# A hybrid decoder trunk whose instructions on all engines but TensorE are ordered by latest times counted back from TensorE's products

## Chip, cores, metric

One core of one Trainium2 chip runs the whole program. The metric is the device time of one execution in microseconds (us), as the median of several.

## The reference

Two layers of a decoder trunk, with 1024 channels and 256 tokens in float32. Each normalises the stream, projects it once to 12832 channels, and feeds three mixers: a Mamba-2 scan behind a causal convolution, attention over a sliding window of 128 with sinks, and attention with a learned forgetting. Each mixer has a SiLU gate and a projection; a sigmoid gate per channel, computed from the input, merges them, and an output projection is added to the stream.

```
h = rms_norm(x, norm_w[l])
u = h @ w_in[l]                       # 1024 x 12832, all branches
ys = [mamba2(conv(xbc), z, dt, ...), swa(rope(q), rope(k), v, z, sinks), fox(q, k, v, f, z)]
g = sigmoid(u_gate + gate_bias[l])    # per branch and channel
x = x + sum(g[b] * (ys[b] @ w_proj[l, b])) @ w_out[l]
...
out = rms_norm(x, final_norm_w)
```

## The kernel before

**Weights.** The weights stream from HBM in 255 parts of at most 512 KB (128 partitions x 1024 numbers), all started by SyncE (`load_part`, L366). ScalarE rounds each part to TensorE's fast format (`hi`, L290), VectorE subtracts to get what is left (`lo`, L291), and TensorE adds three products, hi x hi, lo x hi and hi x lo (`mm`, L109). In the head, parts are split in halves (`w_high` L1470, `w_low` L1476). Six raw parts and six split ones fit; `feed` lets at most four split parts be held ahead of TensorE.

**Work of TensorE.** Every piece of the program is a function that issues the products of one set of columns, and then calls `pump`, which lets pieces that wait (`launch`) go on: scans, softmaxes and gate evictions, each with a delay in TensorE time written out by hand (`D_SOFT`, `D_FOLD`, ...). So the order of TensorE's instructions is that of the program text and of these delays. Transposes go through TensorE too (`transpose`, L113). PSUM has three banks `mm` for products and five banks `mx` for the rest.

**Order of the others.** In the head (from L1431) the order on TensorE, VectorE, ScalarE and GpSimd is that of the program text, and behind it only TensorE's is (`manual_schedule`). The rest is placed by the language's scheduler, under hints: `issue_after` (an instruction not ahead of another), `high_priority`, `keep_in_program_order` (here `pin`), and `after_evictions(3, f)`, which puts a piece behind the third eviction from now. Buffers rotate: each tag has so many, taken in turn.

**The head.** SyncE starts the first half of x (two transfers), the first weight part (two), the second part, the second half of x (512 KB, L1433), the third part, the rope table (L1435) and more parts. TensorE transposes x four blocks at a time (`turn`), VectorE multiplies with the norm's weight on the way out (L1457), ScalarE rounds to `hTh` (`high`, L1461), VectorE takes the rest (`low`, L1465); ScalarE also sums the squares (`square`, L241). The first product is that of the attention's keys (`keys`).

**What else the steps touch.** In a sliding-window quad (four heads, `swa_quad`, `attn_quad`) VectorE masks scores and takes minima (L621 to L642), ScalarE exponentiates (L616), VectorE multiplies by the reciprocal sum (L645), two heads at a time, and TensorE transposes the result. A gate's product is evicted by VectorE with a bias (`u_gate`, L1112), which ScalarE's queue has brought as a broadcast of 256 KB (L1108). A convolution channel (`u_conv`) is evicted by ScalarE in two halves (`dma_sum`, L492 and L493), a transfer that GpSimd starts adds one to the other in SBUF (L494), and then ScalarE reads the sum for the first tap (L832), VectorE for the other three (L835).

## Time and profile before

| | us |
|---|---|
| median of 3 runs | 806.49 (806.43 to 806.95) |
| profiled execution | 806.35 |
| its span | 804.6 |
| TensorE busy | 795.5 |
| VectorE busy | 684.2 |
| ScalarE busy | 534.5 |
| GpSimd busy | 167.6 |

The span runs from the first to the last instruction that the profiler records; 1.75 us of the profiled execution lie around it. Times in the trace count from the start of the span. PE is TensorE's products, PEld its loads of weights, which overlap them; DVE is VectorE, ACT ScalarE, POOL GpSimd, SP SyncE. A name with a q (SPq) is the engine's queue of instructions, where transfers are started.

### The profile page before, as it was taken

How to read it: one execution, taken by the hardware profiler on the slowest of the kernel's cores; microseconds unless marked ns; L12 is line 12 of the kernel's file. 1: busy time of each engine (PE TensorE's matmuls, PEld its weight loads, DVE VectorE, ACT ScalarE, POOL GpSimd, SP SyncE). 2: the span in 40 equal slices, each digit the busy share in tenths (PEclk: the TensorE clock that was granted, in tenths of full speed). 3: DMA queues.
4: the chain of work that ended last, by engine and by line, in shares of the span. 5: the costliest groups of instructions: out<-in, count | busy, mean ns of one | idle time of the engine just before them, and what ended most of it. 6: DMA issues, size and time to landing. Idle time of an engine off the chain costs nothing.

```text
span 804.6 us, 14840 instructions
## 1 busy us (share of the span) xinstructions
PE 795.5 (99%) x5160; PEld 710.4 (88%) x5160; DVE 684.2 (85%) x1416; ACT 534.5 (66%) x1146; POOL 167.6 (21%) x236
## 2 busy tenths in 40 slices
PE   8999999999999999999999999999999999999996
PEld 7999988888998988888998899888889988888896
DVE  6878999997998997795785899999889999969865
ACT  7776768865775885543665688687657768755452
POOL 3066213140220100033001741122311120002000
PEclk9999999999999999999999999999999999999999
DMA  9997987797756565677678987679976546587632
GB/s 309 283 260 178 251 220 201 216 298 219 197 180 169 169 190 174 216 254 206 219 251 259 238 213 211 159 217 283 284 214 204 173 144 202 158 250 208 211 108 77
DMA packets 138826, 170.43 MB, mean 212 GB/s; under 512 B 9352, under 2 KB 106464, under 8 KB 138752
## 3 DMA queue, kind: packets, MB, share of 16 engines
q1 hardware_dynamic: 114960, 140.53, 56.0%
q0 software_dynamic: 13328, 13.29, 10.5%
q10 hardware_dynamic: 10464, 15.67, 6.8%
q8 instruction: 41, 0.67, 0.3%
q14 instruction: 33, 0.27, 0.1%
HBM read 154.71 MB, written 2.16 MB: 195 GB/s over the span
## 4 chain that ended last, share of the span: by engine, by line
PE 96%; DVE 2%; DMA 1%; issue 1%; ACT 1%; SPq 0%; DVEq 0%; ACTq 0%
PE mm L109 83%; PE mx L109 9%; PE mx L113 3%; DMA raw<-in_w_in_dram 1%; DVE lo L291 0%; DVE L L1112 0%; DVE pp L621 0%; ACT hi L290 0%; DVE L L835 0%; SPq L366 0%; SPq L189 0%; DVE L L949 0%; DVE mx L629 0%; DVE L L1457 0%; ACT pp L616 0%
## 5 line engine op out<-in xcount | busy, mean ns | idle before, releaser
L109 PE MATMUL mm<-L,hi 128*128 128x512 f32 x1056 | 354.5, 387 | 0.2
L291 DVE TENSOR_TENSOR lo<-raw,hi 128x1024 fp32r<-128x1024 f32 (+1 forms) x276 | 313.2, 1153 | 40.9 <-ACT hi L290 36.1
L109 PE MATMUL mm<-hi,L 128*128 128x512 f32 (+2 forms) x1168 | 302.9, 349 | 0.1
L290 ACT ACTIVATE hi<-raw 128x1024 fp32r<-128x1024 f32 (+1 forms) x276 | 265.9, 983 | 51.1 <-PE mm L109 35.7
L109 PE MATMUL mm<-L,lo 128*128 128x256 f32 x1056 | 266.6, 273 | 0.0
L109 PEld LDWEIGHTS mm<-hi,L 128*128 128x128 f32 x1168 | 205.9, 190 | 22.9 <-issue 1.5
L109 PEld LDWEIGHTS mm<-L,hi 128*128 128x128 f32 x1056 | 195.1, 190 | 26.8 <-issue 2.4
L109 PEld LDWEIGHTS mm<-L,lo 128*128 128x128 f32 x1056 | 202.1, 191 | 5.3
L109 PE MATMUL mm<-lo,L 128*128 128x512 f32 (+2 forms) x584 | 201.3, 347 | 0.0
L109 PEld LDWEIGHTS mm<-lo,L 128*128 128x128 f32 x584 | 110.2, 190 | 11.0 <-DVE lo L291 0.3
L494 POOL DMA_DIRECT2D L<-L x68 | 60.9, 917 | 191.6 <-ACT L L493 139.5
L1080 POOL TENSOR_SCALAR_AFFINE_SELECT bias<-bias 128x128 f32<-128x128 f32 x64 | 31.9, 531 | 83.3 <-DMA bias<-cumd 82.1
L835 DVE SCALAR_TENSOR_TENSOR L<-L,vec,L 128x255 f32<-128x255 f32 (+2 forms) x96 | 46.2, 482 | 1.5
L492 ACT ACTIVATE L<-mm 128x256 f32<-128x256 f32 x84 | 32.1, 383 | 19.3 <-PE mm L109 13.9
L658 ACT ACTIVATE pp<-pp,nm 128x128 f32<-128x128 f32 x64 | 28.3, 443 | 22.9 <-DVE nm L652 22.9
L1115 ACT ACTIVATE L<-L 128x512 f32<-128x512 f32 x24 | 15.1, 631 | 34.5 <-DVE L L1112 30.7
L494 POOL DMA_DIRECT2D qt<-L x16 | 14.2, 926 | 71.8 <-ACT qt L493 65.0
L616 ACT ACTIVATE pp<-pp,nm 128x128 f32<-128x128 f32 x32 | 12.6, 394 | 24.4 <-DVE nm L621 23.6
L493 ACT ACTIVATE L<-mm 128x256 f32<-128x256 f32 x68 | 26.3, 387 | 2.0 <-DMA L<-L 2.0
L1148 POOL TENSOR_TENSOR L<-L,L 128x512 f32<-128x512 f32 x8 | 12.0, 1495 | 74.0 <-DVE L L1147 74.0
L1112 DVE TENSOR_TENSOR L<-mm,L 128x512 f32<-128x512 f32 x22 | 15.1, 687 | 11.1 <-PE mm L109 11.1
L841 ACT ACTIVATE L<-L 128x256 f32<-128x256 f32 x32 | 13.4, 418 | 16.1 <-DVE L L835 16.0
(213 smaller groups left out, 916.6 us busy)
## 6 DMA issues: line engine op xcount, KB each, us to landing
raw<-in_w_in_dram SPq DMA_DIRECT2D x191, 512.0 KB, 5.1
raw<-in_w_proj_dram SPq DMA_DIRECT2D x48, 512.0 KB, 6.1
L<-L POOLq DMA_DIRECT2D x72, 128.0 KB, 5.6
raw<-in_w_out_dram SPq DMA_DIRECT2D x16, 512.0 KB, 5.3
bias<-cumd ACTq DMA_DIRECT2D x16, 256.0 KB, 3.5
L<-cumd ACTq DMA_DIRECT2D x8, 512.0 KB, 5.9
L<-in_gate_bias_dram ACTq DMA_DIRECT2D x12, 256.0 KB, 5.2
qt<-L POOLq DMA_DIRECT2D x16, 128.0 KB, 6.0
```

The costliest lines, as they stand in the source:

```text
L109: nc.tensor.matmul(o, a, b, **kw)
L113: nc.tensor.transpose(o, a, i)
L290: keep(act)(hi, src, AF.Copy)
L291: keep(tt)(lo, src, hi.bitcast(F32), op=ALU.subtract)
L492: act(halves(lo), ordered(p[:, S:2 * S]), AF.Copy)
L493: last = act(halves(out), ordered(p[:, 0:S]), AF.Copy)
L494: nc.gpsimd.dma_start(out, lo, accum_op=ALU.add)
L658: act(pp[:, i, sl], pp[:, i, sl], AF.Exp, scale=-1.0, bias=nm[:, e:e + 1], accum_out=sums[:, e:e + 1])
L835: stt(a[:, s:S], x_[:, 0:S - s], y.vec[:, 16 * j + u:16 * j + u + 1], a[:, s:S], op0=ALU.mult, op1=ALU.add)
L1080: nc.gpsimd.affine_select(out=bias[:, i, dst], in_=bias[:, i, src], compare_op=ALU.is_ge, fill=NEG, base=0, pattern=[[-1, P]], channel_mul ...
L1112: tt(halves(g), p, halves(y.gb), op=ALU.add)
L1115: finish(act(g, g, AF.Tanh, scale=0.5))
```

## The change

The program text stays, but `nc` is now a recorder: every call adds an `Op` with what it reads and writes, and nothing is issued. At the end `order_of` gives each op a latest time, counted back from the times at which TensorE would do its products if it never waited (`deadlines`). It then plays all five engines through with a time for each kind of instruction and transfer (`Op.cost`, `run`): at each step an engine takes, of the ops that can start first, the one with the earliest latest time. A buffer goes to who is ready first, in the slot that is free first. Behind the first 16 us an op steps back if another with an earlier time would be held up by it (`guarded`). The loop runs four times, with TensorE's times taken anew from the last round. `emit` then issues everything in the order found, on all engines by hand, so every instruction has line 461, and each slot is a tile of its own.

The hints `issue_after`, `high_priority` and `keep_in_program_order` are gone. The identity matrix is made by a memset and a select instead of a helper that does the same. TensorE's instructions and their order are the same in both kernels, as are the numbers of the other engines' compute instructions. The core of the diff:

```diff
+def deadlines(ops, before, end):
+    for op in ops:
+        op.late = op.nominal + op.busy if op.engine == "tensor" else end + 50.0
+    for op in reversed(ops):
+        op.due = min(op.nominal, op.late - op.busy) if op.engine == "tensor" else op.late - op.busy
+        for d in op.deps:
+            o = ops[d]
+            o.late = min(o.late, op.due - (3.0 if o.dma else o.lag))
...
+            c = [(max(r, free[e]), op) for r, op in c if r is not None]
...
+            t0 = min(r for r, _ in c)
+            r, op = min(((r, op) for r, op in c if r <= t0 + 1e-9), key=lambda x: (x[1].due, x[1].i))
+            if e != "tensor" and not forced and t0 > OPENING:
+                until = guarded(e, t0, op)
...
+        if op.dma:
+            wire = max(wire, op.end + 0.8) + op.kb / 330
+            op.land = max(wire + 1.0, op.end + 2.2)
...
+    with tc.manual_schedule(engines={ENG.PE, ENG.DVE, ENG.Activation, ENG.Pool, ENG.SP}):
+        for op in order:
...
+            getattr(getattr(nc, op.engine), op.name)(*map(real, op.args), **{k: real(v) for k, v in op.kw.items()})
...
-        with tc.issue_after(out.ins):
+        if True:
             for _ in range(len(ends_later)):
                 ends_later.pop(0)()
...
-                with tc.high_priority():
+                if True:
...
-    with tc.manual_schedule(engines={ENG.PE}):
-        for g in late:
-            g()
-        for i, f, last in ops[3:]:
-            run_op(i, f, last)
+    for g in late:
+        g()
+    for i, f, last in ops[3:]:
+        run_op(i, f, last)
+
+    bufs_of = {tag: n for tag, (_, n, _, _) in nc.space.items()}
+    emit(nc, order_of(nc, bufs_of, verbose=VERBOSE), tc, pools)
```

Three places where the order moves. The first is ScalarE's queue in the head. Before, from the first square on (`ss` takes the sums; `L8_23_128` is `hTh`, the rounded x; `hi_...` the weight parts):

```order
L241 ACTIVATE L2_36_141,ss_25_130<-L8_3_68 128x512
L1461 ACTIVATE L8_23_128<-L8_22_127 128x512
L1470 ACTIVATE hi_26_131<-raw_12_99 128x512 x2
L1461 ACTIVATE L8_23_128<-L8_22_127 128x512
L1470 ACTIVATE hi_28_133<-raw_13_102 128x512 x2
L241 ACTIVATE L2_41_209,ss_25_130<-L8_3_68 128x512
L1461 ACTIVATE L8_23_128<-L8_22_127 128x512 x2
L1470 ACTIVATE hi_30_135<-raw_15_107 128x512 x2
L241 ACTIVATE L2_42_247,ss_25_130<-L8_3_68 128x512
L241 ACTIVATE L2_43_249,ss_25_130<-L8_3_68 128x512
```

And now, where `L8_2_2_132` is `hTh` and `in_gate_bias_dram` the gate's bias in HBM:

```order
L461 ACTIVATE tab_0_0_67<-tab_0_0_67 128x1
L461 ACTIVATE L2_1_0_111,ss_0_0_112<-L8_0_0_69 128x512
L461 ACTIVATE L8_2_2_132<-L8_1_1_125 128x512
L461 ACTIVATE L2_2_1_139,ss_0_0_112<-L8_0_0_69 128x512
L461 ACTIVATE hi_0_0_153<-raw_0_0_86 128x512
L461 DMA L2_3_10_162<-in_gate_bias_dram 128x512
L461 ACTIVATE hi_0_0_153<-raw_0_0_86 128x512
L461 ACTIVATE L8_2_2_132<-L8_1_1_125 128x512
L461 ACTIVATE hi_1_1_184<-raw_1_1_97 128x512 x2
L461 ACTIVATE L2_4_2_207,ss_0_0_112<-L8_0_0_69 128x512
L461 ACTIVATE L2_5_3_217,ss_0_0_112<-L8_0_0_69 128x512
L461 ACTIVATE L8_2_2_132<-L8_1_1_125 128x512
```

The sums of the second half of x (`L2_4_2_207`, `L2_5_3_217`) moved from behind both L1461 of that half to ahead of them, and a gate-bias transfer now stands between the halves of the first high copy. A first such transfer stands further ahead, as ScalarE's third instruction, behind the transfer of norm_w; before, the first is the 31st row of the queue. On GpSimd the transfers of the small constants of both layers now alternate with the masks right behind the identity; before, those of layer 0 alone stand there, behind the masks and the root of L224. On SyncE the rope table moved back by three weight parts.

The second place is VectorE's queue in layer 0 around the end of the fourth sliding-window quad and the eviction of the second token half of a gate. Before (`pp_399_1959` and `pp_400_1960` are the two pairs of heads, `L2_426_2086` the gate):

```order
L1112 TENSOR_TENSOR L2_411_2031<-mm_398_1946,L2_397_1944 128x512
L644 RECIPROCAL rsum_408_2009<-sums_402_1962 128x4
L642 TENSOR_TENSOR sums_402_1962<-sums_402_1962,es_409_2012 128x4
L645 TENSOR_TENSOR pp_399_1959<-pp_399_1959,rsum_408_2009 128x2x256
L644 RECIPROCAL rsum_410_2016<-sums_402_1962 128x4
L645 TENSOR_TENSOR pp_400_1960<-pp_400_1960,rsum_410_2016 128x2x256
L949 SCALAR_TENSOR_TENSOR L8_184_909<-L1_412_2034,L8_184_909 128x256
L291 TENSOR_TENSOR lo_421_2069<-raw_373_1841,hi_420_2068 128x1024
L291 TENSOR_TENSOR lo_424_2081<-raw_376_1855,hi_423_2080 128x1024
L291 TENSOR_TENSOR lo_439_2143<-raw_390_1918,hi_438_2142 128x1024
L1112 TENSOR_TENSOR L2_426_2086<-mm_413_2037,L2_397_1944 128x512
L291 TENSOR_TENSOR lo_442_2157<-raw_393_1932,hi_441_2156 128x1024
```

And now (`pp_1_7_2082` is the second pair, `L2_5_12_2120` the gate, `vec_0_0_937` the taps' weights):

```order
L461 TENSOR_TENSOR es_1_7_2075<-nm_1_3_2004,nsink_0_0_316 128x4
L461 SCALAR_TENSOR_TENSOR L1_2_102_1979<-L1_5_94_1920,vec_0_0_937,L1_2_102_1979 128x255
L461 SCALAR_TENSOR_TENSOR L1_6_96_1905<-L1_12_86_1796,vec_0_0_937,L1_6_96_1905 128x253
L461 SCALAR_TENSOR_TENSOR L1_2_102_1979<-L1_5_94_1920,vec_0_0_937,L1_2_102_1979 128x254
L461 TENSOR_TENSOR lo_2_50_2089<-raw_2_50_1812,hi_2_50_2072 128x1024
L461 TENSOR_TENSOR lo_3_51_2098<-raw_3_51_1851,hi_3_51_2087 128x1024
L461 TENSOR_TENSOR sums_1_3_2017<-sums_1_3_2017,es_1_7_2075 128x4
L461 SCALAR_TENSOR_TENSOR L1_2_102_1979<-L1_5_94_1920,vec_0_0_937,L1_2_102_1979 128x253
L461 TENSOR_TENSOR L2_5_12_2120<-mm_1_41_2056,L2_3_10_162 128x512
L461 RECIPROCAL rsum_3_7_2128<-sums_1_3_2017 128x4
L461 TENSOR_TENSOR lo_4_52_2130<-raw_4_52_1889,hi_4_52_2109 128x1024
L461 TENSOR_TENSOR pp_1_7_2082<-pp_1_7_2082,rsum_3_7_2128 128x2x256
```

The first pair's multiplication (`pp_0_6`) stands five rows ahead of these. The second pair's moved from ahead of three splits to behind three, and taps of the convolution stand among them; the gate's eviction moved from behind the third of these splits to behind the second. All four quads of a layer show the same: the first pair is multiplied before the second's minima have all been taken, and the second pair follows behind splits and taps.

The third place is ScalarE's queue at the first tap of a convolution channel in layer 0. Before, the eviction of `L1_227_1100`, to which the transfer adds, stands seven rows ahead of these, and the last row reads it:

```order
L290 ACTIVATE hi_252_1234<-raw_208_1025 128x816
L1045 ACTIVATE L8_64_331<-mm_244_1170 128x136
L1046 ACTIVATE L8_64_331<-mm_244_1170 128x120
L948 ACTIVATE L1_245_1197<-L8_184_909 128x256
L290 ACTIVATE hi_256_1254<-raw_220_1076 128x816
L290 ACTIVATE hi_278_1360<-raw_223_1090 128x544
L290 ACTIVATE hi_281_1374<-raw_238_1147 128x1024
L1045 ACTIVATE L8_64_331<-mm_248_1209 128x136
L1046 ACTIVATE L8_64_331<-mm_248_1209 128x120
L832 ACTIVATE L1_255_1248<-L1_227_1100,vec_180_898 128x256
```

And now, where the second row is the eviction of `L1_7_53_1150` and the last one reads it:

```order
L461 ACTIVATE L1_5_52_1144<-mm_0_21_1111 128x256
L461 ACTIVATE L1_7_53_1150<-mm_0_21_1111 128x256
L461 ACTIVATE L4_0_0_1156<-mx_1_14_1141 128x512
L461 ACTIVATE hi_0_30_1166<-raw_0_30_933 128x1024
L461 ACTIVATE L1_11_57_1174<-L8_0_6_967 128x256
L461 ACTIVATE L1_9_58_1181<-L8_0_6_967 128x256
L461 ACTIVATE L1_0_55_1186<-mm_2_22_1148 128x256
L461 ACTIVATE L1_1_56_1190<-mm_2_22_1148 128x256
L461 ACTIVATE hi_1_31_1195<-raw_1_31_963 128x816
L461 ACTIVATE L1_6_59_1208<-L1_7_53_1150,vec_0_0_937 128x256
```

Between eviction and reader 15 rows stood before, and 7 stand now.

More of the change, by code (lines that the diff above doesn't have):

```diff
@@ L9 @@
 from concourse._compat import with_exitstack
-from concourse.masks import make_identity
 F32 = mybir.dt.float32
@@ L47, with __init__ @@
 C_G = 9760
+ENG = mybir.EngineType
+ENGINES = ("tensor", "vector", "scalar", "gpsimd", "sync")
+FIRST_WRITES = ("out", "accum_out")
+SLIP, OPENING = 0.05, 16.0
+class Buf:
+    def __init__(self, tag, shape, dtype, space):
+        self.tag, self.shape, self.dtype, self.space = tag, list(shape), dtype, space
+        self.on_p = space != "dram"
+        free = shape[1:] if self.on_p else shape
+        self.n = int(np.prod(free)) if len(free) else 1
+        self.ap = None
+        self.turn = None
+        self.users, self.open, self.last = [], 0, 0.0
+        self.writer = np.full((4, self.n), -1, np.int32)
+        self.pe_reader = np.full((4, self.n), -1, np.int32)
+        self.readers = []
@@ new lines, in finish_of, with order_of @@
+def finish_of(op):
+    return op.land if op.dma else op.end + op.lag
+def order_of(rec, bufs_of, rounds=4, verbose=False):
+    ops = rec.ops
+    by_tag = {}
+    for b in rec.bufs:
+        by_tag.setdefault(b.tag, []).append(b)
+    for op in ops:
+        op.behind = [d for d in op.behind - op.deps if ops[d].engine != "tensor" or op.engine != "tensor"]
+        op.deps = sorted(op.deps)
+        for d in op.deps:
+            ops[d].after.append((op, True))
+        for d in op.behind:
+            ops[d].after.append((op, False))
+    before = {}
+    for tag, bs in by_tag.items():
+        n = bufs_of[tag]
+        for a, b in zip(bs, bs[n:]):
+            before[id(b)] = a
+    t = 0.0
+    for op in ops:
+        if op.engine == "tensor":
+            op.nominal = t
+            t += op.busy
+    end = t
+    for _ in range(rounds):
+        deadlines(ops, before, end)
+        end, before = run(ops, by_tag, bufs_of)
+        t = 0.0
+        for op in ops:
+            if op.engine == "tensor":
+                t = op.start if op.start < OPENING else t
+                op.nominal = t
+                t += op.busy
+        end = t + 8.0
+        if verbose:
+            print("end", round(end, 1))
+    return sorted(ops, key=lambda op: (op.start, op.i))
@@ L190, in hybrid_trunk @@
     ident = T("ident", [P, P])
-    make_identity(nc, ident)
+    nc.gpsimd.memset(ident, 0.0)
+    nc.gpsimd.affine_select(out=ident, in_=ident, compare_op=ALU.not_equal, fill=1.0, base=0,
+                            pattern=[[-1, P]], channel_multiplier=1)
     tri = T("tri", [P, P])
@@ L881, in ssd_group @@
         decs = []
-        with tc.issue_after(own.ins):
+        if True:
             ds = T("ds", [P, 4], bufs=2)
@@ L1427, in tables @@
                 act(cs[32 * r:32 * r + 32, i, :], p[src, 0:S], AF.Copy)
-    ENG = mybir.EngineType
-    with tc.manual_schedule(engines={ENG.PE, ENG.DVE, ENG.Activation, ENG.Pool}):
+    if True:
         load_to(2)
```

328 lines of the change are left out of this document (307 added, 21 removed).

## Prediction

> **What bounds the kernel now.** I read the page first, then the busy time of each engine by stretch (head, body, tail), then the waits of TensorE, then the chain of waits. The page's first line gives the span, and the stretches give TensorE's share in each.
>
> ```profile
> span 804.6 us, 14840 instructions
> ```
>
> Columns of the next rows: stretch, its length, busy us of PE, PEld, DVE, ACT and POOL, granted clock, DMA share, GB/s.
>
> ```profile
> 0.00:12.64 12.64, 10.19 (x63) 8.57 (x63) 7.44 (x14) 7.70 (x15) 2.36 (x15) 1.00 0.86 275
> 12.64:798.30 785.66, 785.34 (x5098) 701.86 (x5098) 674.41 (x1395) 525.94 (x1130) 165.20 (x221) 1.00 0.74 212
> 798.30:804.60 6.30, 0.00 (x0) 0.00 (x0) 2.38 (x9) 0.82 (x2) 0.00 (x0) 0.69 0.22 83
> ```
>
> TensorE works 785.34 of the 785.66 us between 12.64 and 798.30. It idles 2.45 us ahead of that and 6.30 us behind it; in the body 0.32 us. The change leaves TensorE's instructions and their order as they are, so all that it can give is these idle times, and all that it can cost is new ones. Its waits by releaser:
>
> ```profile
> PE mx L113 <- POOL ident masks.py:199: 1.5, 1, 1.5
> PE mx L113 <- DMA L<-in_x_dram: 0.3, 1, 0.3
> PE mx L109 <- ACT hi L1470: 0.3, 2, 0.2
> ```
>
> All three are in the head. The chain of waits there (start, us, what) shows which transfer sets the moment from which TensorE runs through:
>
> ```profile
> 2.69 5.61 DMA raw<-in_w_in_dram
> ...
> 10.02 0.45 PE mx L113 x4
> 10.47 0.02 issue
> 10.50 0.70 DVE L L1457
> 11.20 0.02 issue
> 11.22 0.64 ACT L L1461
> 11.87 0.04 issue
> 11.91 0.71 PE mm L109 x4
> ```
>
> The second weight part lands at 2.69 + 5.61 = 8.30, TensorE works on it until 10.02, then transposes the second half of the tokens; VectorE and ScalarE turn these into operands, and at 11.91 the first of the long products starts. From there on TensorE has no slack, so whatever moves 11.91 moves the end by as much.
>
> The profiled execution took 806.35 us, 0.14 under the median of the runs shown, 806.49. I make the sum in differences, and lay it on the median.
>
> **The head.** In the new order ScalarE starts two gate-bias transfers of 256 KB in the opening (behind norm_w, and between the two halves of the first high copy); before, the first of them starts at 23.5 us (last row below). GpSimd starts the small transfers of both layers at once, where before those of layer 0 start behind the root. SyncE's order is the same but for the rope table, moved back behind three weight parts. What these meet:
>
> ```profile
> 3.21 0.50 SPq L1433 DMA_DIRECT2D L<-in_x_dram  x1
> L<-in_x_dram SPq DMA_DIRECT2D x1, 512.0 KB, 6.4
> DMA packets 2641, 2.87 MB, mean 358 GB/s; under 512 B 98, under 2 KB 2402, under 8 KB 2641
> L<-in_gate_bias_dram ACTq DMA_DIRECT2D x1, 256.0 KB, 6.1
> L1108 ACTq DMA_DIRECT2D L<-in_gate_bias_dram x12: 334/352/444, 23.5 to 741.6; - x12
> ```
>
> The third row is the traffic of 8 to 16 us, when the DMA engines are busy throughout. The second half of x, issued at 3.21, lands at 3.21 + 6.4 = 9.6. At 358 GB/s each 256 KB (262 thousand bytes) takes 0.73 us from whoever is behind it. The first gate-bias transfer is issued ahead of the weights and of x; the second at about 7 us, and a landing 6.1 us after the issue, as the fourth row has it, would let most of it share the engines while x is under way. I count both in full, 1.46 us: x at 11.07.
>
> The small transfers have a price in two adjacent stretches, of which the second is when before's eight of layer 0 land:
>
> ```profile
> 18.00:20.00 2.00, 2.00 (x21) 2.00 (x20) 1.95 (x2) 2.00 (x8) 2.00 (x5) 1.00 1.03 365
> 20.00:22.00 2.00, 2.00 (x20) 2.00 (x19) 1.12 (x1) 2.00 (x3) 0.52 (x1) 1.00 1.00 242
> ```
>
> The DMA share stays at 1.00 while the rate falls from 365 to 242 GB/s: 246 thousand bytes less in 2 us, worth 0.67 us at 365. Of the new thirteen, those issued by 5 us can land ahead of x, perhaps half of them. Bounds 0 and 0.67; I take 0, since the first ones are issued behind the masks and weights already stand in the queue, and keep 0.67 for the range.
>
> Then ScalarE. Both squares of the second token half now stand ahead of L1461 of that half; before, they come later.
>
> ```profile
> L241 ACT ACTIVATE L<-L x14: 398/616/632, 3.8 to 796.3; 128x512 f32<-128x512 f32 x8, 128x256 f32<-128x256 f32 x6
> L241 ACT ACTIVATION_READ_ACCUMULATOR L<-L x14: 184/188/190, 4.4 to 796.9; 128x1 f32 x14
> ```
>
> A square with its read of the sum is 0.62 + 0.19, less some overlap: 0.75, two of them 1.5. They wait for x, so they end at 11.07 + 1.5 = 12.57, and L1461 follows there and not at 11.22: **+1.35 us**. VectorE's part isn't later: the transposes need x at 11.07 too, + 0.48 + 0.70 makes 12.25. With only the first transfer in the way x lands at 10.33, the squares end at 11.83: +0.6. With the small transfers as well: +2.0. With the early transfers free: 9.6 + 1.5 = 11.1, which 11.22 covers: 0. So 0 to +2.0.
>
> [...]
>
> **The body.** There VectorE is what TensorE stands closest to.
>
> ```profile
> 45.00:190.00 145.00, 144.81 (x1002) 129.72 (x1002) 130.98 (x288) 104.50 (x258) 50.92 (x63) 1.00 0.89 236
> 100.00:152.00 52.00, 51.81 (x366) 45.45 (x365) 50.31 (x131) 39.05 (x103) 10.92 (x14) 1.00 0.75 203
> 200.00:300.00 100.00, 100.00 (x742) 89.40 (x741) 94.35 (x252) 74.36 (x181) 14.40 (x28) 1.00 0.65 185
> ```
>
> Between 100 and 152 us VectorE is busy 50.31 of 52. There TensorE loses 0.19 of its 0.32 us, at two places of that stretch: the transposes of a quad's probabilities, and a product behind a gate's eviction.
>
> ```profile
> 123.08 0.69 DVE L645 TENSOR_TENSOR pp<-pp,rsum 128x512 f32<-128x512 f32 x1
> 123.92 0.63 PE L113 MATMUL mx<-ident,pp 128*128 128x128 f32 x4
> 129.62 0.60 PE L113 MATMUL mx<-ident,pp 128*128 128x128 f32 x4
> 145.48 0.69 DVE L645 TENSOR_TENSOR pp<-pp,rsum 128x512 f32<-128x512 f32 x1
> 146.09 0.42 DVE L949 SCALAR_TENSOR_TENSOR L<-L,L 128x256 f32<-128x256 f32 x1
> 146.50 3.50 DVE L291 TENSOR_TENSOR lo<-raw,hi 128x1024 fp32r<-128x1024 f32 x3
> 149.91 0.68 DVE L1112 TENSOR_TENSOR L<-mm,L 128x512 f32<-128x512 f32 x1
> 150.74 1.33 PE mm L109 x7
> ```
>
> The first pair of heads is normalised until 123.77 and transposed at 123.92: no slack. The second pair is wanted 5.7 us later. Before, VectorE does both pairs of a quad together; the new order finishes the first, and puts two splits and some taps ahead of the second. That is some 2 us less work ahead of the first (minima, sums and taps that now follow it, at 0.15 to 0.5 us each, and here and there a split of 1.2), and 2 to 4 us more ahead of the second, two or three splits and taps, inside its 5.7. At 150, the product at 150.74 waits for the eviction that ends at 150.59; before it, three splits take 3.50 us. In the new order two splits stand there, 1.2 us less. Both stalls go, and so do their like in layer 1: **-0.32 us**, all the idle time of the body and no more. Bounds -0.32 and 0.
>
> The other moves in the body I cost at nothing, as long as VectorE's covers hold: bias evictions behind other evictions on ScalarE, slots taken by who is free first, the removed waits on launches. What they could cost is the second rival.
>
> **The tail** runs after TensorE's last product in the same order on VectorE, ScalarE and SyncE: 0.
>
> **Sum:** +1.35 - 0.32 = +1.03, so 806.49 + 1.03 = 807.5 us (the profiled execution would give 806.35 + 1.03 = 807.4). A difference under 0.2%, 1.6 us, can't be told from no change here: the sides begin below 804.9 and above 808.1.
>
> **The rivals.**
>
> *Free transfers.* The early ones fill gaps in the wire, and x lands as before; the head costs 0 to 0.3, the body gains 0.3 (or what refilling costs beyond it): 806.2. For it: from the start to 12.64 us the rate is 275 GB/s, under the 358 of later, so there may be room. Against: a DMA share of 0.86 in that stretch, which includes the first 2 us without any data. Chance 0.17.
>
> *ScalarE caught by accumulating transfers* (the slower side). A tap's operand is evicted by ScalarE, added to by a transfer that GpSimd starts, and read by ScalarE (L832).
>
> ```profile
> L<-L POOLq DMA_DIRECT2D x72, 128.0 KB, 5.6
> L290 ACT ACTIVATE hi<-raw 128x1024 fp32r<-128x1024 f32 (+1 forms) x276 | 265.9, 983 | 51.1 <-PE mm L109 35.7
> ...
> L492 ACT ACTIVATE L<-mm 128x256 f32<-128x256 f32 x84 | 32.1, 383 | 19.3 <-PE mm L109 13.9
> ```
>
> Landing takes 5.6 us from the issue. Before, 15 other instructions of ScalarE stand between eviction and reader at the first such place; in the new order 7: two high copies of about 1 us and five evictions or scalings of about 0.4, 4.0 us in all. So ScalarE may stand 1.6 us there, with splits and exponentials queued behind it. It idles 145.0 - 104.5 = 40.5 us from 45 to 190, so sixteen such waits per layer, 26 us, would fit; but VectorE behind it has only 1.7 us to give from 100 to 152, and it decides from there: two waits of 1.6 that VectorE can't fill pass 1.5 us on, three 3.1. At 0 to 3.1 per layer, say 1.0, it is +2.0 on top of the head: 809.5, and 813.7 at worst. Against it: splits run several parts ahead of TensorE, and the first pair of each quad gains 2 us of slack. Chance 0.31.
>
> *It does nothing where it counts.* TensorE has the same list; if the others' new orders shift only waits that nobody waits for, and the head's second square hides, the time is 806.5. Chance 0.07.
>
> **How the numbers follow.** My forecast has 0.45: 806.2 (head 0, body -0.32) to 808.5 (head +2.0), most of it within 0.2%, a quarter above. Faster by over 0.2% needs 1.6 us; the body has 0.32 and the head's 2.45 contain the wait for the first data, so 0.04. Slower: 0.45 x 0.25 + 0.31 x 0.9 = 0.39, with a little of the rest 0.40. Same: 0.56. The range runs from 805.8, which leaves room for refilling times that the busy rows hide, to 810.3, into the slower rival's middle.
>
> **What would show it.** Right: the second half of x lands at 11 us or later, two L241 run directly behind it, L1461 ends after 12.9, TensorE's long stretch starts at 13.2 to 13.3 and has no idle time at the quads; VectorE's L1112 near 150 has two splits ahead of it. Wrong: x still lands at 9.6 (free transfers); or TensorE waits in the body on VectorE or ScalarE for over 0.5 us, with ScalarE's L832 waiting on DMA ahead of it (second rival). A time below 804.9 would mean that TensorE's own busy time, the same instructions, had shrunk.

## The result, and the profile after

| | before | after |
|---|---|---|
| median, us | 806.5 (806.43 to 806.95, 6 runs) | 842.23 (839.96 to 846.75, 6 runs) |
| profiled execution | 806.35 | 846.75 |
| its span | 804.6 | 845.0 |
| mean granted clock | 0.998 | 0.984 |

The ratio is 1.0451 (1.0417 to 1.0485): 35.7 us slower, where +1.0 was forecast and 810.3 was the end of the range. The profiled execution of after is the slowest of its six, which spread over 6.8 us.

The first lines of its page, to be held against the span of 804.6 and VectorE's 684.2 and ScalarE's 534.5 of before:

```profile
span 845.0 us, 14837 instructions
...
PE 813.4 (96%) x5160; PEld 720.5 (85%) x5160; DVE 687.0 (81%) x1416; ACT 540.2 (64%) x1146; POOL 170.0 (20%) x236
```

VectorE, ScalarE and GpSimd do the same work in almost the same time (1.4% more at most). TensorE's busy time has grown from 795.5 to 813.4 with the same products, and it idles 31.6 us instead of 9.1. So there are two things to find: who makes TensorE wait, and why its products last longer.

The waits of after (engine, what it stands in front of, who releases it; us in total, times, longest):

```profile
ACT L L461 <- DMA L<-L: 41.7, 26, 3.2
...
PE mx L461 <- DVE nm L461: 17.1, 6, 4.6
...
DVE L L461 <- DMA L<-L: 13.0, 8, 4.9
```

And the waits of before for the same transfers on these two engines, all that there are:

```profile
DVE L L557 <- DMA L<-L: 3.8, 2, 2.6
...
ACT L L492 <- DMA L<-L: 2.4, 1, 2.4
...
ACT L L493 <- DMA L<-L: 2.0, 2, 1.3
...
ACT L L832 <- DMA L<-L: 0.6, 1, 0.6
```

`L<-L` are transfers that GpSimd starts, most of them the adding ones. ScalarE stood 5.0 us on them before and 41.7 now, VectorE 3.8 and 13.0. TensorE stands 17.1 us on `nm`, VectorE's minima over the scores of a sliding-window quad; in before it never waits for them. These six waits are the largest new ones. How one comes about, in after, in order of start (start, duration, what; in brackets the idle time ahead of it and its releaser):

```profile
66.25 0.76 DVE L461 TENSOR_TENSOR L<-L,cs 128x256 f32<-128x256 f32 x2 [4.86 <-DMA L<-L]
...
69.98 1.16 PE L461 MATMUL mx<-L,qt 32*128 32x128 f32 x24
...
71.62 2.35 DVE L461 TENSOR_TENSOR lo<-raw,hi 128x1024 fp32r<-128x1024 f32 x2
75.01 0.43 DVE L461 TENSOR_TENSOR L<-L,cs 128x256 f32<-128x256 f32 x1 [1.05 <-DMA L<-L]
75.36 0.35 DVE L461 CUSTOM_DVE_ANT_0 pp<-mx,wmask,nsink 128x128 f32<-128x128 f32 x1
...
75.77 1.22 PE L461 MATMUL mx<-L,qt 32*128 32x256 f32 x5 [4.62 <-DVE nm L461]
```

The scores of a quad are 32 short products, 16 for each block of 128 tokens; those of both blocks go to the same four PSUM banks. (`pps[0]` and `pps[1]` are these two blocks, and not two pairs of heads, as the texts ahead of the result call them.) TensorE does the first 24 and then stands 4.62 us, until VectorE has read the first block's scores out of a bank in which the next products write other columns. VectorE comes to that reading late, behind a rope step (`L<-L,cs`, L557 of before) that stood 4.86 us on a transfer, splits, and a rope step that stood 1.05. In before, all 32 go through at once, and VectorE's reading 3.3 us behind them holds nobody:

```profile
65.66 1.59 PE L109 MATMUL mx<-L,qt 32*128 32x128 f32 x32
...
70.58 0.34 DVE L621 CUSTOM_DVE_ANT_0 pp<-mx,wmask,nsink 128x128 f32<-128x128 f32 x1
```

So the lateness itself isn't new. VectorE's first reading starts 2.7 to 5.5 us behind the start of a quad's scores in the eight quads of before (4.92 in this one), and 1.6 to 5.4 us behind it in after (5.38 in this one). New is that TensorE waits for it, in six of the eight quads.

One reason why the products last longer shows right behind that pause. Columns: stretch, its length, busy us of PE, PEld, DVE, ACT and POOL, granted clock, DMA share, GB/s.

```profile
74.00:76.00 2.00, 0.23 (x1) 0.24 (x2) 0.97 (x5) 0.26 (x1) 0.56 (x1) 0.50 1.05 167
76.00:78.00 2.00, 2.00 (x11) 1.26 (x12) 0.70 (x5) 0.93 (x5) 0.00 (x0) 0.50 1.08 267
78.00:80.00 2.00, 2.00 (x8) 1.72 (x8) 2.00 (x11) 0.68 (x5) 0.00 (x0) 0.50 0.92 240
80.00:82.00 2.00, 2.00 (x12) 1.80 (x11) 1.05 (x2) 1.05 (x2) 0.00 (x0) 0.84 0.07 15
```

The clock falls to half during the pause and stays there for some 5 us of work behind it. Summed over the trace, TensorE's busy time at half clock holds 10.8 us less work than at full clock (in before: nothing; its 0.998 comes from the 6.3 us behind the last product). That explains 10.8 of the 17.9 us by which the busy time has grown. The other 7.1 are not the clock's. Busy time also grows at full clock where TensorE is stopped often and briefly, as in e3_both below (the kernel with the landing corrected and the early transfers held; it has no busy time at half clock):

```profile
PE 800.1 (98%) x5160; PEld 712.9 (88%) x5160; DVE 683.7 (84%) x1416; ACT 543.3 (67%) x1146; POOL 164.3 (20%) x236
```

That is 4.6 us more than before, and 4.5 more than e8_both, below, which has the same order on every engine without these stops (795.6). So a stop cost more here than the idle time that the waits list for it; why, is not shown.

Where the time is lost along the run, by the start of the same product in both traces:

| before, us | after, us | lag | place |
|---|---|---|---|
| 11.91 | 13.63 | 1.72 | first long product |
| 20.33 | 24.67 | 4.34 | end of the head |
| 66.64 | 75.77 | 9.13 | first quad |
| 136.35 | 151.54 | 15.20 | last quad of layer 0 |
| 226.01 | 244.55 | 18.54 | later in layer 0 |
| 461.33 | 487.11 | 25.78 | first quad of layer 1 |
| 485.21 | 517.11 | 31.89 | a later quad of layer 1 |
| 531.04 | 567.05 | 36.01 | last quad of layer 1 |
| 751.09 | 791.39 | 40.31 | near the end |

This is the profiled execution of after, 4.5 us above the median. Some 4.3 us go in the head, most of the rest in the steps around the quads: 4.34 to 15.20 in layer 0, 18.54 to 36.01 up to the last quad of layer 1. The tail behind the last product is 6.3 us in both.

The head in after:

```profile
11.51 0.63 ACT L461 ACTIVATE L<-L 128x512 f32<-128x512 f32 x1 [0.50 <-DMA L<-in_x_dram]
...
12.14 0.61 ACT L461 ACTIVATE L<-L 128x512 f32<-128x512 f32 x1
...
12.95 0.63 ACT L461 ACTIVATE L<-L 128x512 fp32r<-128x512 f32 x1
...
13.63 1.44 PE L461 MATMUL mm<-hi,L 128*128 128x256 f32 x8
...
15.06 0.63 ACT L461 ACTIVATE hi<-raw 128x512 fp32r<-128x512 f32 x1 [1.48 <-DMA raw<-in_w_in_dram]
...
16.27 0.49 PE L461 MATMUL mm<-hi,L 128*128 128x256 f32 x2 [0.74 <-ACT L L461]
```

The second half of x is there at 11.51 and two squares stand behind it, as forecast; the first long product starts at 13.63, 1.72 us late. What the forecast did not have is the fifth row: the weights land late as well, and TensorE waits again, 0.74 us at 16.27 and 1.08 at 24.67.

### The profile page after: what moved, and what is told of

It is laid out like the page before. It is cut to its first block, busy times and chain, and to the rows that moved or that the text cites. A ratio compares the mean times of both kernels' runs of the same rounds, so it can differ in the third digit from the quotient of the medians.

```text
span 845.0 us, 14837 instructions
## 1 busy us (share of the span) xinstructions
PE 813.4 (96%) x5160; PEld 720.5 (85%) x5160; DVE 687.0 (81%) x1416; ACT 540.2 (64%) x1146; POOL 170.0 (20%) x236
## 4 chain that ended last, share of the span: by engine, by line
PE 65%; DMA 6%; issue 5%; DVE 4%; ACT 3%; POOL 1%; ACTq 0%; POOLq 0%; DVEq 0%
PE mm L461 55%; PE mx L461 10%; DMA L<-L 4%; DVE L L461 2%; DVE lo L461 2%; DMA L<-cumd 2%; ACT hi L461 1%; ACT L L461 1%; POOL L L461 0%; DMA cumd<-L 0%; POOL qt L461 0%; POOL bias L461 0%; ACTq L461 0%; DVE pp L461 0%; DVE sm L461 0%
## 5 line engine op out<-in xcount | busy, mean ns | idle before, releaser
L461 DVE TENSOR_TENSOR lo<-raw,hi 128x1024 fp32r<-128x1024 f32 (+2 forms) x292 | 330.8, 1150 | 57.1 <-ACT hi L461 48.6
L461 ACT ACTIVATE hi<-raw 128x1024 fp32r<-128x1024 f32 (+2 forms) x292 | 279.9, 974 | 81.2 <-PE mm L461 59.5
L461 ACT ACTIVATE L<-L 128x256 f32<-128x256 f32 (+2 forms) x184 | 89.5, 504 | 88.5 <-DVE L L461 73.2
L461 PEld LDWEIGHTS mm<-lo,L 128*128 128x128 f32 x584 | 111.1, 191 | 13.2 <-DVE lo L461 2.3
L461 ACT ACTIVATE L<-mm 128x256 f32<-128x256 f32 (+2 forms) x202 | 67.0, 372 | 30.1 <-PE mm L461 26.4
L461 ACT ACTIVATE pp<-pp,nm 128x128 f32<-128x128 f32 (+1 forms) x96 | 40.8, 426 | 32.8 <-DVE nm L461 32.6
L461 DVE SCALAR_TENSOR_TENSOR L<-L,vec,L 128x255 f32<-128x255 f32 (+3 forms) x112 | 52.1, 476 | 10.7 <-ACT L L461 10.4
L461 DVE TENSOR_TENSOR L<-mm,L 128x256 f32<-128x256 f32 (+1 forms) x70 | 37.1, 532 | 24.7 <-PE mm L461 24.3
L461 DVE SCALAR_TENSOR_TENSOR L<-L,L 128x256 f32<-128x256 f32 (+1 forms) x94 | 46.1, 497 | 2.1 <-ACT L L461 1.9
L461 ACT ACTIVATE L<-L,vec 128x256 f32<-128x256 f32 (+1 forms) x48 | 26.7, 568 | 32.8 <-DMA L<-L 32.7
L461 PE MATMUL mx<-L,qt 32*128 32x128 f32 (+1 forms) x256 | 17.3, 369 | 17.1 <-DVE nm L461 17.1
L461 DVE TENSOR_TENSOR L<-L,L 128x512 fp32r<-128x512 f32 (+2 forms) x56 | 32.4, 594 | 1.0 <-ACT L L461 0.7
```

The lines of the kernel that those rows point to most:

```text
L461: getattr(getattr(nc, op.engine), op.name)(*map(real, op.args), **{k: real(v) for k, v in op.kw.items()})
```

## The experiments

Theory A was that the planner's price of a GpSimd transfer is too low. It counts 0.9 us to start it and 2.2 to land, 3.1 in all; the trace has 5.1, as its list of transfers shows (count, size, median us from issue to landing):

```profile
L<-L POOLq DMA_DIRECT2D x72, 128.0 KB, 5.1
```

So readers are put 2 us too near, and ScalarE and VectorE stand there. Theory B was that the losses come from the new order itself, pairs taken apart and slots given to who is first, whatever the landing. Theory C, which came up with the first results, is that TensorE's new waits on a bank are the link by which a late VectorE reaches TensorE.

**The landing.** The planner gets the measured landing, in the play and in the deadlines. Nothing else in it is changed; the order that it finds changes with that.

```diff
+def flight(o):
+    return 4.7 if o.engine == "gpsimd" else 2.2
...
-            o.late = min(o.late, op.due - (3.0 if o.dma else o.lag))
+            o.late = min(o.late, op.due - (flight(o) + 0.8 if o.dma else o.lag))
...
-            op.land = max(wire + 1.0, op.end + 2.2)
+            op.land = max(wire + 1.0, op.end + flight(op))
```

> The changed kernel, with one number of its planner altered: transfers that GpSimd starts are taken to land 4.7 us behind the end of their issue (5.6 behind its start, as in the trace of before) where the planner had 2.2, and the latest time of the issue is moved by the same. Theory A (landing): the body loses its time because readers of the accumulating transfers stand too close, so that VectorE and ScalarE wait on landings (54.7 us in the changed kernel's trace), TensorE waits behind them and then runs at half clock. Then these waits fall below 15 us, TensorE's waits on the quads' minima go from 17.1 to under 3, the granted clock returns to 0.99 or more, and what stays is the head (4.3) and the six small waits of the forgetting attention (4.5): 812 to 819 us. Theory B (order): the losses come from the new order itself, from pairs taken apart and slots given to who is first, and the waits on landings are filled anyway: 832 or more.

820.32 us (819.33 to 823.36), ratio 1.0180 (1.0156 to 1.0204): 21.9 us of the 35.7 are back, a little less than theory A expected, and far more than B left room for. The waits on landings come down to 20.7 us, where under 15 was expected:

```profile
ACT L L465 <- DMA L<-L: 16.7, 10, 4.5
DVE L L465 <- DMA L<-L: 4.0, 7, 1.0
PE mx L465 <- DVE nm L465: 2.9, 6, 0.8
```

TensorE still waits six times for `nm`, but 2.9 us instead of 17.1, and the clock is 0.999. So the waits on a bank are still there, and short when VectorE is punctual: its first reading now comes 1.2 to 2.0 us behind the start of a quad's scores, earlier than in any quad of before.

Which reader is it? Two kernels have the longer landing for one kind of adding transfer only: for those whose sum ScalarE reads first (taps and gates), and for those that VectorE reads first (the rope).

```diff
+    return 4.7 if o.engine == "gpsimd" and o.kw.get("accum_op") is not None and any(f.engine == "scalar" for f, _ in o.after) else 2.2
```

> As e1_landing, but the longer landing is only given to accumulating transfers that ScalarE reads first (taps and gates). Theory A: the stalls from 90 to 155 us and from 505 to 570 go (about 14 us with their slow clock), those of the rotated keys and queries at 70 and 485 us stay: 825 to 832 us. Rival A2, that VectorE's waits alone matter: no gain, 838 or more. Theory B: 838 or more.

```diff
+    return 4.7 if o.engine == "gpsimd" and o.kw.get("accum_op") is not None and not any(f.engine == "scalar" for f, _ in o.after) else 2.2
```

> As e1_landing, but the longer landing is only given to accumulating transfers that VectorE reads first (rotated keys and queries). Theory A: the two stalls of about 4.8 us at 70 and 485 us go with the slow clock behind them (about 15 us in all), those behind taps and gates stay: 824 to 832 us. Rival A2, VectorE's waits alone matter: 812 to 819, as e1_landing. Theory B: 838 or more.

830.21 (828.87 to 831.56) and 832.82 us (830.36 to 835.28, a little above what was expected), two runs each. They give back 12.0 and 9.4 us, 21.4 together, against 21.9 for both: two costs of like size, which add up as far as two runs each, up to 4.9 us apart, can tell. The part of the second rival, ScalarE, is about half of it.

**The head.** On top of the landing, the gate-bias transfers are held until 24 us of the planner's time, and GpSimd's loads of small constants until 17.

```diff
+        self.hold = 0.0
+        if self.dma and not self.reads and engine == "scalar" and self.kb >= 256:
+            self.hold = 24.0
+        if self.dma and not self.reads and engine == "gpsimd":
+            self.hold = 17.0
...
-        t = op.ready
+        t = max(op.ready, op.hold)
```

> As e1_landing, and the planner holds the gate-bias transfers until 24 us and GpSimd's small constants until 17 us of its own time, about when the kernel before starts them. Theory A with the head: the head's 4.3 us go, so it stands 3.5 to 5 us under e1_landing, 808 to 814, and TensorE's long stretch starts near 12 us. Rival: the head's delay is given back later, since the weights then stream ahead: within 1 us of e1_landing.

815.62 us (815.23 to 816.0), ratio 1.0113 (1.0098 to 1.0128): 4.7 us less than with the landing alone, which fits the lag of 4.3 at the end of the head, though the time is above the 808 to 814 expected, as the kernel that it builds on was above its own.

**The waits on a bank.** The third edit makes whoever reads a PSUM bank depend on all products that the program text has written to it so far. So the first block's reading stands behind the second block's products, as in before, and no product waits for a reading in the midst of its bank.

```diff
+        if b.space == "psum" and op.engine != "tensor":
+            op.deps.update(u.i for u in b.users if u.engine == "tensor")
```

Alone, on the changed kernel:

> The changed kernel with one dependency more in its recorder: whoever reads a PSUM bank outside TensorE depends on all products written to that bank so far, as in the order of the program text before. In the changed kernel VectorE's read of the first token block's scores is issued ahead of the last products of the second block into the same bank, and 11 of these products carry a wait on VectorE; here none does, as before. Landings are priced as in the changed kernel (too short). Theory C (bank wait): this new wait is the link by which VectorE's standing on landings reaches TensorE, so TensorE's waits on the minima (17.1 us) go and the time falls to 815 to 826 us, though VectorE and ScalarE still wait about 50 us on landings. Theory A (landings alone): TensorE then waits for the same late VectorE a little further on, at the transposes: 834 us or more.

829.62 us (828.99 to 834.04), ratio 1.0299 (1.0277 to 1.0321): 12.6 us less, between what the two theories expected, so neither holds as it was put. TensorE no longer waits for `nm`, but the landings are as before this edit (ScalarE 46.0 us in 25 waits), and TensorE now meets them elsewhere, as in this row (the engine, the idle time and the releaser in brackets):

```profile
102.22 0.50 PE L463 MATMUL mm<-hi,L 128*128 128x272 f32 x2 [2.47 <-ACT L L463]
```

All three edits together:

> All three alterations: GpSimd's landings at 4.7 us, the early transfers held, and the bank dependency of e4_bank. Theory C: against e3_both (815.6) the waits of the score products (about 5.4 us in six quads) go, and the waits in the forgetting attention too if they are of the same kind (4.5 us): 806 to 811 us. If the order by latest times costs something of its own beside these three causes, it stays above 811.

806.65 us (805.93 to 807.4, 11 runs), ratio 1.000 (0.9992 to 1.0009). The whole loss is accounted for by three causes: landing, head, and waits on a bank.

**The two early kinds of transfer apart.** From the kernel with three edits, one hold at a time is taken back to 0: the gate bias, then the small constants.

```diff
-            self.hold = 24.0
+            self.hold = 0.0
```

> As e5_three, but the two gate-bias transfers start early again, as in the changed kernel. By the prediction's price, 256 KB each at 358 GB/s ahead of x and the squares behind: 0.6 to 1.5 us above e5_three. Rival: nothing, they are free.

```diff
-            self.hold = 17.0
+            self.hold = 0.0
```

> As e5_three, but GpSimd's thirteen small transfers start early again, as in the changed kernel. The changed kernel's head lost 4.3 us where the gate biases explain 1.5, and from 8 to 16 us its mean rate was 264 GB/s with the engines busy: theory: the small transfers cost 2 to 3 us. Rival, the prediction's bound: 0 to 0.67 us.

807.26 us (806.93 to 807.48), +0.61, at the edge of what can be told, and 810.72 us (809.9 to 811.85), +4.07, more than the 2 to 3 expected. Their sum, 4.68, is the 4.7 of the head. The small constants cost nearly seven times what the gate bias costs, though they are far smaller. The first long product of the three kernels, and the only stall of over a microsecond:

```profile
12.42 1.44 PE L472 MATMUL mm<-hi,L 128*128 128x256 f32 x8
```

```profile
13.22 1.44 PE L472 MATMUL mm<-hi,L 128*128 128x256 f32 x8
```

```profile
12.58 1.44 PE L472 MATMUL mm<-hi,L 128*128 128x256 f32 x8
...
24.42 0.49 PE L472 MATMUL mm<-hi,L 128*128 128x256 f32 x2 [2.39 <-ACT L L472]
```

(Three edits; gate bias early; small constants early.) The early gate bias moves the first product by 0.80. One trace of each isn't enough to tell that from scatter (see the squares below): by 200 us the two traces are level, and their spans are equal, 805.6; the 0.61 stands on the medians alone. The small constants leave the first product nearly where it was, and make a hole of 2.39 us at 24.42, where weights are late. The traffic from 8 to 16 us in the two kernels, and in the second the queue of the small transfers (packets, MB, share of the 16 engines' time):

```profile
DMA packets 2410, 2.89 MB, mean 361 GB/s; under 512 B 97, under 2 KB 2155, under 8 KB 2410
```

```profile
DMA packets 1826, 1.83 MB, mean 228 GB/s; under 512 B 204, under 2 KB 1748, under 8 KB 1826
...
q0 software_dynamic: 297, 0.07, 43.5%
```

0.07 MB of small constants take 43.5% of the engines' time there, and the wire carries 1.06 MB less than in the other. The gate bias is 0.26 MB of the 2.89 in that stretch, 0.73 us at 361 GB/s, near the 0.61 that it costs.

**The order of the squares.** With the three edits the first long product is still 0.51 us later than in before (12.42 against 11.91), with the two squares ahead of L1461. Two kernels hold the squares back, so that they stand about where before has them; the second also takes the landing at 5.4.

```diff
+        if engine == "scalar" and "accum_out" in kw and i < 400:
+            Op.squares += 1
+            self.hold = (0.0, 8.5, 13.5, 13.5)[min(Op.squares, 4) - 1]
```

> As e5_three, and the planner holds the sums of squares in the head until 8.5 us (second half of the first tokens) and 13.5 us (second tokens), so that ScalarE's first fourteen instructions stand as in the kernel before. In e5_three's trace TensorE is 0.6 us later than before from the head on, and four stalls in the body of before are gone (0.94 us in all), against 1.0 us of new ones. Expectation: the head's 0.6 goes: 806.0, 0.05 to 0.1% under the kernel before. Rival: the squares in the head cost nothing, the 0.6 us is the transfers' own scatter: 806.6.

```diff
-    return 4.7 if o.engine == "gpsimd" else 2.2
+    return 5.4 if o.engine == "gpsimd" else 2.2
```

> As e7_square, with the landing of GpSimd's transfers at 5.4 us behind the end of the issue instead of 4.7. If waits on landings (11.0 us on ScalarE and 4.2 on VectorE in e5_three) still reach TensorE, it gains up to 0.5 us more: 805.5. If they are covered, it is equal to e7_square within 0.3 us; if readers so far back run into the latest times of what stands behind them, it is slower by up to 1 us.

807.44 (806.83 to 807.99) and 807.36 us (807.02 to 807.86), beside 806.43 of the kernel before on the same chip, both with a ratio of 1.0011 (1.0002 to 1.002): a miss, since 806.0 was expected, and slower than the kernel without this hold if anything. The chain of waits of the first has a place where it loses (start, duration, what):

```profile
11.33 9.37 DMA raw<-in_w_in_dram
...
20.80 0.42 ACT hi L477
...
21.76 0.47 ACT L L477
...
22.27 0.82 PE mm L477 x5
```

A weight part lands at 20.70, ScalarE takes its high copy, and an eviction that TensorE needs stands behind it: 1.2 us of idle time at 22.27, which the kernel without the hold doesn't have. And the hold gave nothing: the first long product starts at 12.50, no earlier than with the squares ahead (12.42). The rival of the expectation, that the squares are free and the transfers scatter, is what the traces show. These are the landings of the second half of x (us from its issue at 3.21) in e3_both and in e8_both (below), where every engine's order is the same, with the squares ahead of L1461:

```profile
L<-in_x_dram SPq DMA_DIRECT2D x1, 512.0 KB, 7.0
```

```profile
L<-in_x_dram SPq DMA_DIRECT2D x1, 512.0 KB, 6.3
```

Their first long products start at 12.55 and 11.76, the second earlier than in before. From this landing to that product it takes 2.1 to 2.3 us, with the squares between (after, e5_three, e3_both, e8_both) or not (before, e7_square). So the landing of x sets this product, the squares cost nothing that shows, and a shift of 0.8 us between two traces can be scatter. The longer landing of GpSimd's transfers changes nothing that can be measured: 4.7 is enough.

**The wait itself, or the moved readings?** The bank edit also moves readings. To see the wait alone, the next kernel keeps the changed kernel's order on every engine, and its slots. Only the sequence in which the five queues are interwoven as instructions are issued is another: a product is issued as soon as all that it needs is, so ahead of a reading that it doesn't need.

```diff
-        for op in order:
+        for op in products_first(rec, order):
```

`products_first` issues TensorE's next instruction if what it depends on and the former tenants of its slot have been issued, and otherwise the one with the earliest planned start. Of TensorE's products, 11 lose a wait on VectorE by it.

> The changed kernel with the same order on every engine, instruction for instruction, and the same slots; only the sequence in which the engines' lists are woven together when issued differs: a product is issued as soon as what it needs has been. So 11 products lose their wait on VectorE's read of another part of the same bank, and nothing else moves. If the bank wait itself is the cost (and not the order that goes with it), it comes near e4_bank, 826 to 834 us; if e4_bank's gain came from the planner's other order, it stays at 840 to 844.

826.57 us (825.58 to 828.73), ratio 1.0244 (1.0227 to 1.0261): 15.7 us less with no order changed. The quad of above in this kernel, TensorE and VectorE:

```profile
70.28 1.59 PE L484 MATMUL mx<-L,qt 32*128 32x128 f32 x32
```

```profile
66.44 0.76 DVE L484 TENSOR_TENSOR L<-L,cs 128x256 f32<-128x256 f32 x2 [5.00 <-DMA L<-L]
...
75.13 0.43 DVE L484 TENSOR_TENSOR L<-L,cs 128x256 f32<-128x256 f32 x1 [0.97 <-DMA L<-L]
75.47 0.34 DVE L484 CUSTOM_DVE_ANT_0 pp<-mx,wmask,nsink 128x128 f32<-128x128 f32 x1
```

VectorE is as late as in after (75.47 against 75.36) and has the same waits on transfers, 5.00 and 0.97. TensorE goes through all 32 products from 70.28 on, where after stood 4.62 us behind the first 24. So the pause there was the wait's, and it arose where a reading was issued ahead of a product of the same bank that it has nothing to do with.

The same weaving, with the landing and the holds:

> The same done to e3_both (815.6 us), where 9 products carry that wait: every engine's order as there. If the waits themselves are the cost: 806 to 810 us, as e5_three. If not: 814 to 817.

806.35 us (805.95 to 806.71, 10 runs), ratio 0.9995 (0.9986 to 1.0005) beside 806.69 of before: the lowest median of all versions, and equal to the kernel before within what can be told. TensorE's waits in it, all there are:

```profile
PE mx L493 <- POOL ident L493: 1.4, 1, 1.4
PE mx L493 <- ACT hi L493: 0.2, 1, 0.2
PE mx L493 <- DVE L L493: 0.2, 1, 0.2
PE mx L493 <- DMA L<-in_x_dram: 0.2, 1, 0.2
```

**The account.** Each cause by runs in which the others are absent: the head 4.7 (by e6_gate and e6_pool; with the waits on a bank present, e3_both from e1_landing gives the same); the landing 826.57 - 806.35 = 20.2, less the head's 4.7, is 15.5; the bank 815.62 - 806.35 = 9.3. That is 29.5 of 35.7 us. The other 6.2, rough as they are beside the spread of after's runs, come only with landing and bank together, which fits that a late VectorE matters most where TensorE waits for it. The clock is part of that: in the profiled executions it is 0.999 without the late landings, 0.995 without the bank waits, and 0.984 with both.

## Why the prediction was right or wrong

**The step from TensorE's unchanged order to a body of "-0.32 and 0": wrong, and the main failure.** The body cost some 31 us instead (35.7 less the head's 4.7): by the account above 15.5 for the late landings, 9.3 for the waits on a bank, and 6.2 for both together. The landings were at least a rival, below; the waits on a bank stood nowhere. TensorE's list is the same, but not what each instruction waits for. The order across the engines decides which side of a shared bank waits: before, the reading waited for both blocks' products; now 11 products wait for a reading. Order on each engine doesn't show this, and the prediction looked only at that. These waits are worth 9.3 us by themselves and up to 15.7 with the late landings (e8_issue). The prediction even counted a companion of this cause as a gain, "the new order finishes the first" block ahead of the second: reading the first block early is what put readings ahead of products. The bank edit and the weaving turn such a wait round, so that the reading waits for the products; no run here left it out, so what would happen without it is not shown.

That "all that it can cost" is new idle times was wrong too: 17.9 us went into a longer busy time, 10.8 of them by the half clock, which the prediction gave no price.

**Head, +1.35: the mechanism held up to the first product, and the term was mis-sized behind it.** x landed at 11.5 (forecast 11.07), two squares ran behind it (1.34 us, forecast 1.5), L1461 started at 12.95 (forecast 12.57), the first product at 13.63 (forecast 13.2 to 13.3). That the squares add to x's delay is not borne out, since the way from x to this product is as long without them. And the step "whatever moves 11.91 moves the end by as much" fails: early transfers delay the weights behind x too, and the head cost 4.7. Of the two transfers, the roles were exchanged. The gate bias, priced at 2 x 0.73, cost 0.61, at the edge of what can be told: about one of the two. That the other found room on the wire is not shown. The small constants, priced at 0 with a bound of 0.67, cost 4.07. That bound was worked out of one stretch of 2 us with eight transfers; in the changed kernel thirteen go out from 1.59 to 10.33 us, through the whole time in which the weights must come, and from 8 to 16 us the rate is 264 GB/s, where before has 358 (228 in e6_pool, where these alone are early). In that stretch of e6_pool they take 43.5% of the engines' time for 0.07 MB.

**Body, -0.32: right for the two places, wrong for the body of the changed kernel,** where the lag grows from 4.34 to 40.31 us by the table above. In the kernels without the three causes the stalls of before are gone. Stretches of e8_both, columns as above; before has 0.19 us of idle time in 100 to 152:

```profile
12.64:120.00 107.36, 107.36 (x795) 98.55 (x796) 94.30 (x218) 84.39 (x207) 44.66 (x62) 1.00 0.96 255
120.00:160.00 40.00, 40.00 (x266) 35.44 (x267) 38.15 (x84) 32.65 (x78) 9.45 (x14) 1.00 0.84 218
```

By the starts of the same products the two places in each layer give 0.22, 0.30, 0.21 and 0.21 us, 0.94 in all and not 0.32; here too, a stop cost more than its idle time (that this is the refilling for which the prediction left room, no run shows). Most of the 0.94 goes elsewhere again (0.33 at 385 us, 0.47 by 450), so that the span is 804.1 against 804.6. That is all the order by latest times brings by itself: nothing that the measurement tells from no change.

**The tail, 0: right.**

**The second rival, ScalarE caught by adding transfers: its mechanism happened, and its price was too small.** It expected sixteen waits per layer of up to 1.6 us; there are 26 in both layers, 1.6 us on average and up to 3.2. It let 0 to 3.1 us per layer through to TensorE; e1_act puts this part at 12.0 us, 6 per layer. And it missed the like on VectorE: the rope reads the sum of such a transfer, and in before `after_evictions(3, turned)` with the hint `issue_after` put that reading three evictions later. Without the hint the planner's 3.1 us decide, and e1_dve puts the difference at 9.4 us. The row of 5.6 us per landing stood in the prediction, and the planner's 2.2 in the diff beside it; they were not compared.

**The first rival (free transfers)** fell with the head. **The third (nothing where it counts)** fell too, though it is what the order itself does once the three causes are out.

**The direction:** no change had 0.56, and slower 0.40, from the head and the second rival; both did make it slower. A loss of 4% was in none of its cases, because in none did TensorE have a wait that the program of before lacks.

## What to carry to other kernels

Where a planner sets the order, hold each of its prices against the trace first: one landing taken 2 us too short cost 15 to 22 us here. With the order of every engine fixed, the sequence in which the queues are woven together still decided who waits for whom at a shared PSUM bank (15.7 us between after and e8_issue): issue the products first, and look for waits of the critical engine that were not there before. Small loads belong behind the stretch in which the wire sets the pace: thirteen of 4 to 32 KB cost 4.07 us there (e6_pool).

## What the runs showed of the hardware

Five pauses of TensorE in after cost more than themselves. The clock went to half with pauses of 4.62, 1.72, 4.58, 2.57 and 1.99 us, for 6.8, 3.4, 6.8, 3.4 and 3.4 us; the stretch around the second, at 149.8 to 151.5, reads:

```profile
151.00:153.00 2.00, 1.46 (x10) 1.04 (x11) 1.20 (x8) 1.29 (x5) 0.86 (x3) 0.83 0.95 262
153.00:155.00 2.00, 2.00 (x6) 1.53 (x6) 2.00 (x13) 1.04 (x7) 0.00 (x0) 0.50 1.00 288
155.00:157.00 2.00, 2.00 (x9) 1.65 (x8) 0.62 (x2) 0.60 (x1) 0.00 (x0) 0.82 0.14 48
```

The clock is short of full by 0.17, 0.50 and 0.18 in these stretches of 2 us, which makes 1.7 us lost in addition to a pause of 1.72. A pause of 1.58 at 102.4 in after, and the one of 2.47 at 99.75 with the bank edit alone, were not followed by it (the clock reads 1.00 in the stretches behind both), though the one of 1.72 was, so the length of a pause doesn't decide it alone.

The trace's record of the clock shows more. Within after, its changes lie whole multiples of 3.413 us apart (6.83 and 3.41 at half clock, 71.68, 331.09, 23.89 and 47.79 between; 331.09 is 97 times 3.413). In the 3.41 us that end at each of the five falls TensorE was idle for 2.66, 1.72, 3.41, 2.57 and 1.73 us. The pause of 1.58 lies within one step of that grid. Where steps of 3.413 us are counted back in e4_bank's trace from its next fall, one of them ends within the pause of 2.47 and cuts it into 0.70 and 1.77. So in after 1.72 us or more idle within a step goes with a fall and 1.58 does not; the 1.77 of e4_bank doesn't fit. What sets the grid, and from how much idle time on the clock falls, is not shown.

Thirteen loads of 4 to 32 KB, 0.07 MB within 8 to 16 us, took 43.5% of the time of the 16 DMA engines in e6_pool, and 1.06 MB less came in that time than in e6_gate.
